# Rotary embedding on one core: tiles of 8, 8, 8, 16, 16 and 8 rows a partition, and rows dealt anew to the engines

## The chip, the cores and the metric

The kernel runs on one core of one Trainium2 chip. The metric is the device time of one execution in microseconds, the median of the runs shown; smaller is better. The profile is of one execution.

## The reference

The input `x` has 16 batches of 512 positions with 1024 numbers each, read as 16 heads of 64. Each head's halves are rotated by the angle of its position:

```python
x = x.reshape(batch, seq, num_heads, head_dim)          # 16, 512, 16, 64
x1, x2 = x[..., :32], x[..., 32:]
cos, sin = cos[None, :, None, :], sin[None, :, None, :]  # cos, sin: 512 x 32
out = concatenate([x1 * cos - x2 * sin, x1 * sin + x2 * cos], axis=-1)
```

All is float32: 33.6 MB are read and 33.6 MB written.

## The kernel before, in words

The 8192 positions are taken as 64 rows of 128 positions. A row is one 4 KB run of `x` in each of the 128 partitions, and a tile is 4 or 8 rows that lie next to each other in a partition, so that a transfer moves one piece of 16 or 32 KB for each partition. `tiles` holds two tiles of 4 rows, six of 8 and two of 4. They go through a ring `x_sb` of 40 rows; results are written over the input and stored from there.

One row `u` takes three steps (L276 to L310):

- `t1 = x * cos` by VectorE into one of three PSUM slots (L293, `mul`);
- `t2 = swapped halves of x * (-sin, sin)` into one of six SBUF buffers, by GpSimd (L257), or by VectorE for the row `V_ROW` of a tile of 8 (L286, flags `V2`);
- `t1 + t2` back into the ring, by VectorE (L304, `comb`), or for the rows flagged in `PE2` by TensorE, which adds t2 to the PSUM slot by a matmul with the identity (L224, four records a row), and ScalarE, which copies the slot into the ring (L191).

VectorE issues the multiply of row u + 1 ahead of the addition of row u (`LEAD`). It may write slot u only when the addition or ScalarE's copy of row u - 3 is done; t2 buffers come free when row u - 6 is added. Everything is ordered by semaphores written out by hand; there is no scheduler.

Of the 64 rows, 58 have their t2 made by GpSimd and 6 by VectorE; 21 are added by TensorE and ScalarE and 43 by VectorE.

Loads are issued by ScalarE (L153): the first 40 rows at once, with the two tables `cos` and `sin` behind the first load, and the other four loads each behind a given row's copy (`LAG`) and after a wait for the store that frees its place in the ring. Stores are issued by SyncE (L161) when a tile's last row is added. Both queues share the 16 DMA engines.

The tables: for tiles of 4 rows the staged `cos` and `sin` can be copied as they are (L264, L182, L183). For tiles of 8 rows a partition holds other positions, and TensorE makes the tables from the staged ones with a picking matrix (L208, two matmuls of 256 columns), which ScalarE copies for GpSimd (L186, L187). VectorE makes its own small sines from PSUM (L271, L272).

Of the kernel before, what the change touches and what calls it, by code (L numbers as in the profile page):

```python
# [6 lines left out]
def bass_split_heads_rope_kernel(  # L7
# [9 lines left out]

    batch, seq, dim = x.shape
    H = int(num_heads)
    HD = dim // H
# [3 lines left out]
    R2 = 2 * R1  # L30
    assert R1 * P == seq and R1 == 4 and batch % 2 == 0
# [8 lines left out]
    singles = (0, 1, batch - 2, batch - 1)  # L40
    tiles = [(b, R1 if b in singles else R2) for b in range(batch) if b in singles or b % 2 == 0]
    NT = len(tiles)
    RING = 5 * R2

    rows = [(t, r) for t, (_, n) in enumerate(tiles) for r in range(n)]
    NU = len(rows)
    EARLY = (NU - RING) // R2


    V_ROW = 3  # L50
    PE2 = [R1 <= u < NU - R1 and u % R2 in (1, 3, 6) for u in range(NU)]
    V2 = [tiles[t][1] == R2 and r == V_ROW for t, r in rows]

# [12 lines left out]
    LAG = 10  # L66

    with ExitStack() as stack:
# [3 lines left out]
        s1_sb = stack.enter_context(nc.sbuf_tensor([P, R1, 2, HALF], fp32))  # L72
        s2_sb = stack.enter_context(nc.sbuf_tensor([P, R2, 2, HALF], fp32))
        ident = stack.enter_context(nc.sbuf_tensor([P, P], fp32))
        pick = stack.enter_context(nc.sbuf_tensor([P, 2, 2, P // 2], fp32))
        zero = stack.enter_context(nc.sbuf_tensor([P, BANK], bf16))
        tab_ps = stack.enter_context(nc.psum_tensor([P, BANK], fp32))
        pair_ps = stack.enter_context(nc.psum_tensor([P, 2, 2, R1, HALF], fp32))
        t1_ps = stack.enter_context(nc.psum_tensor([P, NT1, H * HD], fp32))
        sem_in = [stack.enter_context(nc.semaphore(f"in{t}")) for t in range(NT)]  # L80
        sem_out = [stack.enter_context(nc.semaphore(f"out{k}")) for k in range(EARLY)]
# [3 lines left out]
        sem_c = stack.enter_context(nc.semaphore("ctab"))  # L85
        sem_s = stack.enter_context(nc.semaphore("stab"))
        sem_z = stack.enter_context(nc.semaphore("zero"))
# [7 lines left out]
        sem_t = stack.enter_context(nc.semaphore("pairs"))  # L95
        sem_a = stack.enter_context(nc.semaphore("act"))

        c1_ps = tab_ps[:, 0:R1 * HALF].rearrange("p (r d) -> p r d", d=HALF)
        v_ps = tab_ps[:, R1 * HALF:R1 * HALF + HD].rearrange("p (t d) -> p t d", d=HALF)

        def c_of(t, r):
            return c1_ps[:, r, :] if tiles[t][1] == R1 else pair_ps[:, r // R1, 0, r % R1, :]

        def s_of(t, r):
            return s1_sb[:, r] if tiles[t][1] == R1 else s2_sb[:, r]

        x1 = x.rearrange("b (s r) d -> b s (r d)", r=R1)
        o1 = out.rearrange("b (s r) h d -> b s (r h d)", r=R1)
        x2 = x.rearrange("b s d -> (b s) d").rearrange("(g p r) d -> g p (r d)", p=P, r=R2)
        o2 = out.rearrange("b s h d -> (b s) h d").rearrange("(g p r) h d -> g p (r h d)", p=P, r=R2)  # L110
        xs = x_sb[:].rearrange("p n h t d -> p n (h t d)")

        def in_dram(single, pairs, t):
            b, n = tiles[t]
            return single[b] if n == R1 else pairs[b // 2]

        def in_sbuf(t):
            b, n = tiles[t]
            k = b * R1 % RING
            return x_sb[:, k:k + n].rearrange("p n h t d -> p (n h t d)")  # L120

        def where(u):
            t, r = rows[u]
            return t, r, u % RING

# [6 lines left out]
        def wait_added(eng, u):  # L132

            if n_pe[u]:
                eng.wait_ge(sem_a, n_pe[u])
            if n_comb[u]:
                eng.wait_ge(sem_v, n_comb[u])

        def wait_t2_free(eng, u):

            if u >= NT2:
                v = u - NT2
                if PE2[v]:
                    eng.wait_ge(sem_e, n_pe[v])
                else:
                    eng.wait_ge(sem_v, n_comb[v])

        def stores_of(k):

            return sum(b * R1 // R2 == k for b, _ in tiles)  # L150

        def load(eng, t):
            eng.dma_start(in_sbuf(t), in_dram(x1, x2, t)).then_inc(sem_in[t], 16)  # L153

        def on_sync(sp):
            for u in range(NU):
                t, r, k = where(u)
                if r == tiles[t][1] - 1:
                    wait_added(sp, u)
                    k = u // R2  # L160
                    sp.dma_start(in_dram(o1, o2, t), in_sbuf(t)).then_inc(sem_out[k] if k < EARLY else sem_rest, 16)  # L161
            sp.wait_ge(sem_rest, 16 * sum(stores_of(k) for k in range(EARLY, NU // R2)))

        def on_scalar(ae):
            later = {}
            for t, (b, n) in enumerate(tiles):
                if b * R1 + n <= RING:
                    load(ae, t)
                else:

                    later.setdefault((b * R1 - RING) // R2 * R2 + R2 - 1 + LAG, []).append(t)
                if t == 0:
                    for i, (table, sem) in enumerate(((cos, sem_cos), (sin, sem_sin))):
                        ae.dma_start(stage[:, i, :], table.rearrange("(s r) d -> s (r d)", r=R1)).then_inc(sem, 16)  # L174

            ae.wait_ge(sem_i, 2)
            ae.activation(  # L177
                pick[:], ident[:].rearrange("q (s k) -> q k s", k=2)[:, :, None, :].broadcast_to([P, 2, 2, P // 2]), COPY
            ).then_inc(sem_g, 1)
            ae.wait_ge(sem_sin, 16)  # L180
            sv = stage[:, 1, :].rearrange("s (r d) -> s r d", d=HALF)
            ae.activation(s1_sb[:, :, 0, :], sv, COPY, scale=-1.0)  # L182
            ae.activation(s1_sb[:, :, 1, :], sv, COPY).then_inc(sem_s, 1)  # L183
            ae.wait_ge(sem_t, 2)
            s2 = s2_sb[:].rearrange("p (k r) t d -> p k r t d", r=R1)
            ae.activation(s2[:, :, :, 0, :], pair_ps[:, :, 1, :, :], COPY, scale=-1.0)  # L186
            ae.activation(s2[:, :, :, 1, :], pair_ps[:, :, 1, :, :], COPY).then_inc(sem_s, 1)  # L187
            for u in range(NU):
                if PE2[u]:
                    ae.wait_ge(sem_e, n_pe[u])  # L190
                    ae.activation(xs[:, u % RING, :], t1_ps[:, u % NT1, :], COPY).then_inc(sem_a, 1)  # L191
                for t in later.get(u, ()):
                    k = (tiles[t][0] * R1 - RING) // R2
                    ae.wait_ge(sem_out[k], 16 * stores_of(k))
                    load(ae, t)

        def on_tensor(pe):
# [6 lines left out]
            pe.wait_ge(sem_g, 1)  # L204
            pe.wait_ge(sem_cos, 16)
            pe.wait_ge(sem_sin, 16)
            for k in range(2):
                pe.matmul(  # L208
                    pair_ps[:, k].rearrange("p c r d -> p (c r d)"),
                    pick[:, k].rearrange("q b s -> q (b s)"),  # L210
                    stage[:].rearrange("q c f -> q (c f)"),
                    start=True,
                    stop=True,
                ).then_inc(sem_t, 1)
# [4 lines left out]

# [14 lines left out]
        def on_gpsimd(pl):  # L234
# [10 lines left out]
            ).then_inc(sem_i, 1)  # L245
            for u in range(NU):
                if V2[u]:
                    continue
                t, r, k = where(u)
                if (t, r) == (0, 0):  # L250
                    pl.wait_ge(sem_s, 1)
                if (t, r) == (2, 0):
                    pl.wait_ge(sem_s, 2)
                if r == 0:
                    pl.wait_ge(sem_in[t], 16)
                wait_t2_free(pl, u)
                pl.tensor_tensor(  # L257
                    t2_sb[:, u % NT2, :, :, :], swapped(k), over_heads(s_of(t, r)), mult
                ).then_inc(sem_p, 1)

        def on_vector(ve):
            ve.memset(zero[:], 0.0).then_inc(sem_z, 1)  # L262
            ve.wait_ge(sem_cos, 16)
            ve.tensor_copy(c1_ps, stage[:, 0, :].rearrange("s (r d) -> s r d", d=HALF)).then_inc(sem_c, 1)  # L264
            ve.wait_ge(sem_c, 1)
            ve.wait_ge(sem_w, NT1 * EH)

            def pair_tables():
                ve.wait_ge(sem_s, 2)
                row = pair_ps[:, V_ROW // R1, 1, V_ROW % R1, :]  # L270
                ve.tensor_scalar_mul(v_ps[:, 0, :], row, -1.0).then_inc(sem_c, 1)  # L271
                ve.tensor_copy(v_ps[:, 1, :], row).then_inc(sem_c, 1)  # L272

            first_v = V2.index(True)

            def mul(u):  # L276
                t, r, k = where(u)
                if r == 0:
                    ve.wait_ge(sem_in[t], 16)
                if (t, r) == (2, 0):  # L280
                    pair_tables()
                if u == first_v:
                    ve.wait_ge(sem_c, 3)
                if V2[u]:
                    wait_t2_free(ve, u)
                    ve.tensor_tensor(t2_sb[:, u % NT2, :, :, :], swapped(k), over_heads(v_ps), mult)  # L286
                if u >= NT1:
# [8 lines left out]
                    c_of(t, r)[:, None, :].broadcast_to([P, 2 * H, HALF]),  # L296
# [3 lines left out]
            def comb(u):  # L300
                t, r, k = where(u)
# [3 lines left out]
                    xs[:, k, :],  # L305
# [49 lines left out]
```

## Time and profile before

| what | value |
|---|---|
| median of 3 runs | 161.11 us (161.09 to 161.94) |
| span of the profiled execution, first to last instruction | 160.0 us |
| what lies around the span, against the median | 1.1 us |
| DMA | 67.26 MB, mean 420 GB/s over the span |
| VectorE (DVE) busy | 130.1 us, 81% |
| GpSimd (POOL) busy | 134.9 us, 84% |
| TensorE (PE) matmuls busy | 73.7 us, 46% |
| ScalarE (ACT) busy | 24.4 us, 15% |

The time of the profiled execution itself is not given apart from its span; the runs shown were timed without it. In the profile's lines, PE, PEld, DVE, ACT, POOL and SP are TensorE's matmuls and weight loads, VectorE, ScalarE, GpSimd and SyncE; L257 is line 257 of the kernel. A group's line has its busy time and the mean duration of one instruction, then the engine's idle time just before and what ended it. Durations of neighbours on an engine overlap a little, so the distance between two starts is what one costs. The DMA row gives the busy share of the 16 engines in 40 slices of 4 us, in tenths.

### The profile page before, as it was taken

The page shows a single profiled execution, that of the slowest core. Times are in us where ns is not written, and L with a number is a line of the kernel's source. Part 1 is how long each engine was busy: PE and PEld are TensorE (multiplying, and loading weights), DVE is VectorE, ACT ScalarE, POOL GpSimd, SP SyncE. Part 2 cuts the span into 40 slices and gives each one's busy share as a digit, 9 for nine tenths or more (in the row PEclk, how much of TensorE's full clock was granted, in tenths as well). Part 3 has the DMA queues.
Part 4 walks back from the last instruction along what each step waited for, and adds up shares of the span by engine and source line. Part 5 has one row for each costly group of instructions (what it writes and reads, how often), then busy time and mean ns, then how long its engine had stood idle before and what let it go on. Part 6 is the DMA issues. An engine that isn't in the chain of part 4 may idle for free.

```text
span 160.0 us, 522 instructions
## 1 busy us (share of the span) xinstructions
PE 73.7 (46%) x94; PEld 23.7 (15%) x94; DVE 130.1 (81%) x117; ACT 24.4 (15%) x27; POOL 134.9 (84%) x64
## 2 busy tenths in 40 slices
PE   6050005476427735690948606459439841970000
PEld 1020002021102220220222002002202210320000
DVE  0069998699999998997989709899999989989600
ACT  0420000205020502022022020220220122050000
POOL 1059999999999999999999999698999999289400
PEclk9999999969955865567555685855855599577555
DMA  5999999999999999999999999999999999999997
GB/s 160 401 451 463 401 430 418 410 483 406 401 463 406 494 401 401 483 426 401 467 426 418 410 467 434 401 467 393 420 463 446 418 414 418 479 410 434 414 414 303
DMA packets 3170, 67.26 MB, mean 420 GB/s; under 512 B 352, under 2 KB 608, under 8 KB 608
## 3 DMA queue, kind: packets, MB, share of 16 engines
q10 hardware_dynamic: 1728, 33.69, 49.7%
q1 hardware_dynamic: 1440, 33.56, 48.8%
q14 instruction: 2, 0.02, 0.0%
HBM read 33.69 MB, written 33.55 MB: 420 GB/s over the span
## 4 chain that ended last, share of the span: by engine, by line
DMA 59%; POOL 22%; PE 5%; DVE 3%; issue 2%; ACTq 1%; ACT 1%; DVEq 0%
DMA x_sb<-in_x_dram 41%; POOL t_sb L257 22%; DMA out_dram<-x_sb 18%; PE t_ps L224 5%; DVE x_sb L304 2%; DVE t_ps L293 1%; ACT x_sb L191 1%; ACTq L153 1%; ACTq L174 1%; DVEq L303 0%
## 5 line engine op out<-in xcount | busy, mean ns | idle before, releaser
L257 POOL TENSOR_TENSOR t_sb<-x_sb,s_sb 128x1024 f32<-128x1024 f32 x58 | 134.2, 2358 | 14.2 <-ACT s_sb L183 8.2
L224 PE MATMUL t_ps<-t_sb,ident 128*128 128x512 f32 x84 | 68.9, 973 | 62.8 <-DVE t_ps L293 37.9
L293 DVE TENSOR_TENSOR t_ps<-x_sb,pair_ps 128x1024 f32<-128x1024 f32 x48 | 57.7, 1223 | 9.7 <-ACT x_sb L191 9.7
L304 DVE TENSOR_TENSOR x_sb<-t_ps,t_sb 128x1024 f32<-128x1024 f32 x43 | 52.4, 1218 | 2.1 <-POOL t_sb L257 2.1
L191 ACT ACTIVATE x_sb<-t_ps 128x1024 f32<-128x1024 f32 x21 | 21.5, 1024 | 110.6 <-PE t_ps L224 98.9
L224 PEld LDWEIGHTS t_ps<-t_sb,ident 128*128 128x128 f32 x84 | 21.8, 286 | 109.6 <-DVE t_ps L293 70.0
L293 DVE TENSOR_TENSOR t_ps<-x_sb,tab_ps 128x1024 f32<-128x1024 f32 x16 | 19.3, 1222 | 0.5 <-ACT x_sb L191 0.5
L286 DVE TENSOR_TENSOR t_sb<-x_sb,tab_ps 128x1024 f32<-128x1024 f32 x6 | 7.3, 1212 | 0.0
L264 DVE COPY tab_ps<-stage 128x128 f32<-128x128 f32 x1 | 0.3, 295 | 7.7 <-DMA stage<-in_cos_dram 7.7
L208 PE MATMUL pair_ps<-stage,pick 128*128 128x256 f32 x4 | 2.0, 667 | 5.1 <-DMA stage<-in_sin_dram 5.1
L201 PE MATMUL t_ps<-zero 128*128 128x512 bf16 x6 | 2.7, 630 | 1.3 <-DVE zero L262 1.3
L208 PEld LDWEIGHTS pair_ps<-stage,pick 128*128 128x128 f32 x4 | 1.2, 324 | 6.2 <-issue 6.0
L177 ACT ACT_TABLE_LOAD x1 | 1.3, 1283 | 5.0 <-issue 5.0
L201 PEld LDWEIGHTS t_ps<-zero 128*128 128x128 bf16 x6 | 0.7, 138 | 2.3 <-DVE zero L262 1.2
L262 DVE MEMSET zero<- 128x256 uint32 x1 | 0.3, 272 | 0.9 <-PEq L337 0.9
L182 ACT ACTIVATE s_sb<-stage 128x128 f32<-128x128 f32 x1 | 0.3, 310 | 2.3 <-DMA stage<-in_sin_dram 2.3
L186 ACT ACTIVATE s_sb<-pair_ps 128x256 f32<-128x256 f32 x1 | 0.4, 384 | 1.7 <-PE pair_ps L208 1.7
L235 POOL MEMSET ident<- 128x128 f32 x1 | 0.2, 205 | 0.3 <-POOLq L337 0.3
L177 ACT ACTIVATE pick<-ident 128x256 f32<-128x256 f32 x1 | 0.4, 430 | 0.0
L187 ACT ACTIVATE s_sb<-pair_ps 128x256 f32<-128x256 f32 x1 | 0.4, 377 | 0.0
L237 POOL TENSOR_SCALAR_AFFINE_SELECT ident<-ident 128x128 f32<-128x128 f32 x1 | 0.3, 294 | 0.1
L337 POOL MEMSET const-float32-0.0<- 128x1 f32 x1 | 0.1, 99 | 0.3 <-issue 0.3
(6 smaller groups left out, 1.0 us busy)
## 6 DMA issues: line engine op xcount, KB each, us to landing
x_sb<-in_x_dram ACTq DMA_DIRECT2D x6, 4096.0 KB, 38.1
out_dram<-x_sb SPq DMA_DIRECT2D x6, 4096.0 KB, 25.3
x_sb<-in_x_dram ACTq DMA_DIRECT2D x4, 2048.0 KB, 22.4
out_dram<-x_sb SPq DMA_DIRECT2D x4, 2048.0 KB, 14.9
stage<-in_cos_dram ACTq DMA_DIRECT2D x1, 64.0 KB, 7.6
stage<-in_sin_dram ACTq DMA_DIRECT2D x1, 64.0 KB, 7.3
```

Source lines behind the costliest of these rows:

```text
L153: eng.dma_start(in_sbuf(t), in_dram(x1, x2, t)).then_inc(sem_in[t], 16)
L174: ae.dma_start(stage[:, i, :], table.rearrange("(s r) d -> s (r d)", r=R1)).then_inc(sem, 16)
L177: ae.activation(pick[:], ident[:].rearrange("q (s k) -> q k s", k=2)[:, :, None, :].broadcast_to([P, 2, 2, P // 2]), COPY).then_inc(sem_g, 1)
L186: ae.activation(s2[:, :, :, 0, :], pair_ps[:, :, 1, :, :], COPY, scale=-1.0)
L191: ae.activation(xs[:, u % RING, :], t1_ps[:, u % NT1, :], COPY).then_inc(sem_a, 1)
L201: pe.matmul(t1_ps[:, k, b * BANK:(b + 1) * BANK], zero[:, 0:P], zero[:], start=True, stop=True).then_inc(sem_w, 1)
L208: pe.matmul(pair_ps[:, k].rearrange("p c r d -> p (c r d)"), pick[:, k].rearrange("q b s -> q (b s)"), stage[:].rearrange("q c f -> q (c f)"),
L224: ins = pe.matmul(t1_ps[:, u % NT1, b * BANK:(b + 1) * BANK], ident[:], t2[:, b * BANK:(b + 1) * BANK], start=False, stop=True, skip_group ...
L257: pl.tensor_tensor(t2_sb[:, u % NT2, :, :, :], swapped(k), over_heads(s_of(t, r)), mult).then_inc(sem_p, 1)
L286: ve.tensor_tensor(t2_sb[:, u % NT2, :, :, :], swapped(k), over_heads(v_ps), mult)
L293: ve.tensor_tensor(t1_ps[:, u % NT1, :].rearrange("p (h d) -> p h d", d=HALF), x_sb[:, k, :, :, :].rearrange("p h t d -> p (h t) d"), c_of ...
L304: ve.tensor_tensor(xs[:, k, :], t1_ps[:, u % NT1, :], t2_sb[:, u % NT2, :, :, :].rearrange("p h t d -> p (h t d)"), add,).then_inc(sem_v, 1)
```

## The change

Tiles are now given in a list: rows, place in the ring, the pieces in which the tile is loaded and stored, and the stores that must have landed before it is loaded. The tiles have 8, 8, 8, 16, 16 and 8 rows. The first is loaded in two halves, the second tile of 16 is stored in two halves, and so is the last. The 16-row transfers have pieces of 64 KB for each partition. There are 7 loads of `x` and 8 stores, where there were 10 of each. The two late loads, of 16 and 8 rows, are issued by ScalarE behind rows 27 and 39.

All tables, for tiles of 8 and of 16 rows, are made by TensorE: 12 matmuls of 128 columns, 4 of them for the size of 8, with two picking matrices from ScalarE. The raw sines are written into the third PSUM slot of `t1_ps`, and VectorE reads its own from there, for both sizes, just before its multiply of row 2.

VectorE makes t2 for rows 3 and 6 of a tile of 8 and for rows 3 and 11 of a tile of 16, 12 in all; GpSimd makes 52. TensorE and ScalarE add every odd row from 3 to 59, 29 rows; VectorE adds 35.

```diff
-    singles = (0, 1, batch - 2, batch - 1)
-    tiles = [(b, R1 if b in singles else R2) for b in range(batch) if b in singles or b % 2 == 0]
-    RING = 5 * R2
+    TILES = (
+        (8, 0, (4, 4), (8,), ()),
+        (8, 8, (8,), (8,), ()),
+        (8, 16, (8,), (8,), ()),
+        (16, 24, (16,), (16,), ()),
+        (16, 0, (16,), (8, 8), (0, 1)),
+        (8, 16, (8,), (4, 4), (2,)),
+    )
+    RING = 40
+    BEHIND = {5: 27, 6: 39}
...
-    V_ROW = 3
-    PE2 = [R1 <= u < NU - R1 and u % R2 in (1, 3, 6) for u in range(NU)]
-    V2 = [tiles[t][1] == R2 and r == V_ROW for t, r in rows]
+    V_ROWS = {8: (3, 6), 16: (3, 11)}
+    V2 = [r in V_ROWS[TILES[t][0]] for t, r in rows]
+    PE2 = [2 <= u < NU - R1 and u % 2 == 1 for u in range(NU)]
...
+        raw_sin = {
+            n: t1_ps[:, NT1 - 1, i * BANK:i * BANK + n * HALF].rearrange("p (r d) -> p r d", d=HALF)
+            for i, n in enumerate(SIZES)
+        }
...
         def on_scalar(ae):
...
+            for n in SIZES:
+                m = n // R1
+                ae.activation(
+                    pick[n][:],
+                    ident[:].rearrange("q (s k) -> q k s", k=m)[:, :, None, :].broadcast_to([P, m, m, P // m]),
+                    COPY,
+                ).then_inc(sem_g, 1)
+            for i, n in enumerate(SIZES):
+                ae.wait_ge(sem_t, i + 1)
+                ae.activation(s_sb[n][:, :, 0, :], raw_sin[n], COPY, scale=-1.0)
+                ae.activation(s_sb[n][:, :, 1, :], raw_sin[n], COPY).then_inc(sem_s, 1)
             for u in range(NU):
                 if PE2[u]:
                     ae.wait_ge(sem_e, n_pe[u])
-                    ae.activation(xs[:, u % RING, :], t1_ps[:, u % NT1, :], COPY).then_inc(sem_a, 1)
-                for t in later.get(u, ()):
-                    k = (tiles[t][0] * R1 - RING) // R2
-                    ae.wait_ge(sem_out[k], 16 * stores_of(k))
-                    load(ae, t)
+                    ae.activation(xs[:, place_of(u), :], t1_ps[:, u % NT1, :], COPY).then_inc(sem_a, 1)
+                for i in late:
+                    if BEHIND[i] == u:
+                        for j in TILES[loads[i][0]][4]:
+                            ae.wait_ge(sem_out[j], 16)
+                        load(ae, i)
...
         def on_tensor(pe):
...
+            pe.wait_ge(sem_w, NT1 * EH)
+            for n in SIZES:
+                for c, to in enumerate((c_ps[n], raw_sin[n])):
+                    for k in range(n // R1):
+                        ins = pe.matmul(
+                            to[:, k * R1:(k + 1) * R1, :].rearrange("p r d -> p (r d)"),
+                            pick[n][:, k].rearrange("q b s -> q (b s)"),
+                            stage[:, c, :],
+                            start=c == 0,
+                            stop=True,
+                            skip_group_check=c == 1,
+                        )
+                ins.then_inc(sem_t, 1)
...
         def on_vector(ve):
             ve.memset(zero[:], 0.0).then_inc(sem_z, 1)
-            ve.wait_ge(sem_cos, 16)
-            ve.tensor_copy(c1_ps, stage[:, 0, :].rearrange("s (r d) -> s r d", d=HALF)).then_inc(sem_c, 1)
-            ve.wait_ge(sem_c, 1)
             ve.wait_ge(sem_w, NT1 * EH)
+            def own_sines():
+                ve.wait_ge(sem_s, len(SIZES))
+                for n in SIZES:
+                    v = V_ROWS[n]
+                    some = raw_sin[n][:, v[0]:v[-1] + 1:max(1, v[-1] - v[0]), :]
+                    ve.tensor_scalar_mul(v_ps[n][:, :, 0, :], some, -1.0).then_inc(sem_k, 1)
+                    ve.tensor_copy(v_ps[n][:, :, 1, :], some).then_inc(sem_k, 1)
+                ve.wait_ge(sem_k, 2 * len(SIZES))
             def mul(u):
...
+                if n not in seen:
+                    seen.add(n)
+                    ve.wait_ge(sem_t, SIZES.index(n) + 1)
+                if u == NT1 - 1:
+                    own_sines()
```

## The prediction

> **What bounds the kernel now.** I read the page, then the windows, the DMA view of two stretches, the chain, and the timeline for durations. On the page the DMA engines are busy in every slice but the first and the last:
>
> ```profile
> span 160.0 us, 522 instructions
> ...
> DMA  5999999999999999999999999999999999999997
> ```
>
> The windows (busy us of PE, PEld, DVE, ACT, POOL, then TensorE's clock, DMA share, GB/s) give the rate:
>
> ```profile
> 0.00:4.00 4.00, 2.74 (x6) 0.74 (x6) 0.27 (x1) 0.00 (x0) 0.70 (x6) 1.00 0.57 160
> ...
> 60.00:80.00 20.00, 12.56 (x15) 3.71 (x13) 18.63 (x17) 3.27 (x4) 20.00 (x10) 0.59 1.01 436
> 80.00:100.00 20.00, 10.07 (x11) 3.53 (x12) 14.50 (x14) 2.87 (x3) 19.74 (x9) 0.59 1.00 431
> ...
> 156.00:160.00 4.00, 0.00 (x0) 0.00 (x0) 0.00 (x0) 0.00 (x0) 0.00 (x0) 0.50 0.71 303
> ```
>
> At 433 GB/s (the mean of 60 to 100 us) one row of a tile (128 x 4 KB, 0.52 MB), in or out, takes 1.21 us. The first window moved 0.64 MB, 1.5 us of work, so transfers in effect begin at 2.5 us; 67.26 MB at 433 is 155.3 us; the last window falls 1.2 us short, the slowest of the 16 engines ending last. 2.5 + 155.3 + 1.2 = 159.0 of the 160.0. The bytes stay the same, so the change can gain about 1 us at most, and loses whatever time both queues stand empty. GpSimd and VectorE are close behind:
>
> ```profile
> L257 POOL TENSOR_TENSOR t_sb<-x_sb,s_sb 128x1024 f32<-128x1024 f32 x58 | 134.2, 2358 | 14.2 <-ACT s_sb L183 8.2
> ...
> L293 DVE TENSOR_TENSOR t_ps<-x_sb,pair_ps 128x1024 f32<-128x1024 f32 x48 | 57.7, 1223 | 9.7 <-ACT x_sb L191 9.7
> ```
>
> The chain ends in a load, then that load's four rows:
>
> ```profile
> 93.17 47.21 DMA x_sb<-in_x_dram
> ...
> 140.45 9.30 POOL t_sb L257 x4
> ```
>
> How the two queues share the engines is in the DMA view of 22 to 36 us (q10 loads in 32 KB pieces, q1 stores in 16 KB pieces) and of 60 to 100 us (both 32 KB):
>
> ```profile
> q10 hardware_dynamic: 143, 4.16, 71.2%
> q1 hardware_dynamic: 109, 1.79, 29.7%
> ```
>
> ```profile
> q1 hardware_dynamic: 301, 8.81, 51.2%
> q10 hardware_dynamic: 292, 8.52, 49.4%
> ```
>
> Shares go by piece size, 2.3 to 1 and about 1 to 1. Piece durations come from the timeline:
>
> ```profile
> 36.62 1.98 PE L224 MATMUL t_ps<-t_sb,ident 128*128 128x512 f32 x4 [0.18 <-DVE t_ps L293]
> ...
> 58.59 3.78 PE L224 MATMUL t_ps<-t_sb,ident 128*128 128x512 f32 x4 [3.61 <-DVE t_ps L293]
> ...
> 144.57 1.22 DVE L293 TENSOR_TENSOR t_ps<-x_sb,tab_ps 128x1024 f32<-128x1024 f32 x1
> 145.70 1.22 DVE L304 TENSOR_TENSOR x_sb<-t_ps,t_sb 128x1024 f32<-128x1024 f32 x1
> ```
>
> VectorE starts one operation every 1.13 us; GpSimd's x4 in 9.29 us gives 2.31 a row; a TensorE row takes 1.98 us at full and 3.78 at half clock, its ScalarE eviction 1.02.
>
> **Rows dealt anew.** GpSimd 58 to 52 rows (-6 x 2.31 = -13.9 us), TensorE 21 to 29, VectorE 64 + 43 + 6 = 113 operations to 64 + 35 + 12 = 111 (-2.3 us). Per 8 rows: in 8-row tiles VectorE 8 + 4 + 2 = 14 x 1.13 = 15.8 us is the limit (GpSimd 6 x 2.31 = 13.9); in a 16-row tile only two rows leave GpSimd, 7 x 2.31 = 16.2 per 8, as before. Before, 8 rows took 16.0 to 17.3 us between its stores (30.8, 46.8, 63.5, 80.8). So the pace hardly changes.
>
> **Tables.** Before, VectorE's first multiply starts at 9.19 and GpSimd's at 9.62. Now 12 matmuls of 128 columns stand ahead; the nearest row is L208, two matmuls of 256 columns in 2.05 us, so between 0.43 (cost by column) and 0.85 each (by instruction). I take 0.55, nearer the first, as the weight loads (0.32) overlap. Size 8 is ready at 9.1 + 4 x 0.55 + 0.2 = 11.5, GpSimd starts at 12.2 after two ScalarE copies of 0.38 (+2.6). Size 16 at 16.0, copies of about 0.6 each (estimated from 128, 256 and 1024 elements: 0.30, 0.38, 1.02), then four small VectorE operations: the third multiply at about 17.5 against 13.2 (+4.3; bounds +3 and +8). No transfer waits for that at first: 40 rows of loads are queued by 5 us.
>
> **Stores.** Twelve VectorE operations after 17.5 and TensorE's last row put store 0 (rows 0-7) at about 35; before, two 4-row stores went at 20.3 and 30.8. Stores 1 and 2 follow at 51 and 67. The engines stay full: loads alone until about 36 (28 rows). Of the first 40, the last 12 rows, in 64 KB pieces beside 32 KB stores, take two thirds: 12 x 1.21 x 1.5 = 22 us, so the first 16-row tile lands at 60 (1.5 us for the slowest engine, a little more than the 1.2 above). Loads and stores 0 and 1 are 56 rows, 2.5 + 67.8 = 70.3: store 2 at 67 is just in time. This is thin: tables at their upper bound put 3 us of nothing there.
>
> **The late loads on ScalarE.** They were there before. The 16-row load stands behind row 27 (about 74), when stores 0 and 1 have landed (72 to 73), so ScalarE is not held, where before the same wait held VectorE part of 9.7 us. Its issue (0.33, at worst the 1.94 us that one took before) holds only the next eviction; the 8-row load behind row 39 is alike.
>
> **One 16-row load in place of two 8-row loads.** This decides. Before, rows 40-47 landed at 92.0 and rows 48-55 at 111.3. Now no row of 40-55 is free until all 16 are in, and by then 56 rows of loads and 24 of stores have moved: 2.5 + 80 x 1.21 = 99.3, + 1.5 = 100.8. Row 39 is done at 60 + 14 x 2.31 + 4.9 = 97.2 (its TensorE row and eviction at half clock, hand-overs); its 16-row store then takes half of the engines from the load's tail, +0.5 to +3 us. Take 101.8 (bounds 100.8 and 104). VectorE and GpSimd stand idle from about 93: 9 us, as much as the 9.7 before, but now with nothing to make it up. Then 14 rows of GpSimd (32.3) and TensorE's row 55 (4.9): 139.0. The last 8 rows are VectorE's, 16 x 1.13 = 18.1, some three of them done already: +15.0, 154.0. The last 4-row store found queued stores ahead of it before and took 8.8 from issue to landing; the quickest 4-row transfer took 7.8; here 8.0: 162.0. While row 55 is awaited the transfers run out of work for 2 or 3 us, which is where the loss shows.
>
> **Sum.** 101.8 + 37.2 + 15.0 + 8.0 = 162.0 against 160.0: +2.0. The median of the runs is 161.1, 1.1 over the span; 162.0 + 1.1 = 163.1. By the bounds (100.8 to 104, and 0.5 either way for VectorE) 161.6 to 165.8, nearly all above 162.
>
> **Rivals.**
> B, no starving: TensorE runs at full clock. It would be busy 3.6 of every 4.1 us, against 12.6 of 20 at a clock of 0.59 between 60 and 80. Row 55 comes 1.8 earlier, the transfers stay full, and the end is that of the bytes, 159.0 to 160.2, so 160.1 to 161.3, say 161.0: not slower. Against it, row 39 and its store come earlier as well and delay the 16-row load by about as much. It decides if rows 40 to 63 take under 51 us from a landing near 101.
> C, larger pieces are faster. 22 to 36 us, with 16 KB stores, ran at 425 GB/s, 60 to 100 at 433. A like step from 32 to 64 KB on the 48 of 128 rows that get such pieces (two loads and a store of 16) is 1.9% of 58 us, 1.1 us: 160.0. Against it, 8 to 12 us, 16 KB loads alone, ran at 451. [...]
> D, a 64 KB piece is moved as two of 32 KB. Shares are 1 to 1, the first 16-row tile lands at 67 instead of 60, row 39 comes 7 us later, at 104, the 16-row load is issued at 81, and the queues stand empty for about 6 us: 159.6 + 6 + 1.1 = 166.7. [...]
>
> **How the numbers follow.** Forecast 0.59, B 0.23, C 0.04, D 0.14. 0.5% is 0.8 us, about what a measurement can tell; faster is below 160.3, same up to 161.9. Faster 0.04 (C), same 0.22 (B, but for a little of it), slower 0.74. The range, 161.0 to 165.5, leaves out C, the lower part of B and D.
>
> **What would show it.** After: the sixth x load landing 101 to 104 with GpSimd's and VectorE's longest waits ended by it; stores at about 35, 51, 67, 97; a DMA slice under 9 near 139 to 142; q10 to q1 at 2 to 1 while 64 KB pieces meet 32 KB. GpSimd busy 52 x 2.36 = 123. I am wrong if the slices stay at 9 to the end (B), or already dip near 80 and 102 (D).

## The result: 167.6 us, 3.9% slower, and the profile after

The changed kernel takes 167.62 us (median of 6 runs, 166.81 to 168.38) beside 161.38 for the kernel before in the same comparison: a ratio of 1.039, 95% interval 1.0365 to 1.0415. The forecast was slower, 163.1 us (161.0 to 165.5): the sign is right, the size 4.5 us short, outside the range. The profiled execution took 166.81 us, the quickest of the six, with a span of 165.6.

The page of the kernel after, its span and its DMA row:

```profile
span 165.6 us, 615 instructions
...
DMA  5999999979999888999899999999999998799995
```

A slice is 4.1 us. The engines are nearly always busy, as before; the two thin slices at 137 to 145 us are the forecast idle time. (A piece is booked whole in the slice in which it starts. The slices of 7 and 8 before 100 us come from that: laid out over their durations, the DMA records leave no idle time there, a busy share of 1.00 to 1.02 in each slice from 4 to 99 us.) But busy is not moving. The windows of the kernel after (busy us of PE, PEld, DVE, ACT and POOL, then TensorE's clock, DMA share, GB/s):

```profile
60.00:100.00 40.00, 20.28 (x36) 7.45 (x36) 31.62 (x28) 9.22 (x9) 32.41 (x14) 0.91 1.01 433
...
100.00:135.00 35.00, 16.52 (x28) 6.05 (x28) 27.90 (x25) 6.15 (x6) 29.55 (x13) 0.76 1.00 407
...
136.00:143.00 7.00, 3.95 (x5) 1.47 (x6) 4.83 (x5) 1.42 (x2) 7.00 (x4) 0.76 0.65 281
```

From 60 to 100 us they move the 433 GB/s of before; from 100 to 135 they are as busy (1.00) and move 407, where the kernel before moved 430 in the same stretch:

```profile
100.00:135.00 35.00, 20.23 (x26) 5.69 (x24) 33.88 (x31) 7.17 (x7) 32.93 (x15) 0.69 1.00 430
```

That is 35 x (1 - 407/433) = 2.1 us of work left undone by engines that never rest. Then, from 136 to 143, the queues do run dry (281): 7 x (1 - 281/433) = 2.5 us, as much as the forecast idle time of 2 or 3 us. The groups and waits of the kernel after:

```profile
L284 POOL TENSOR_TENSOR t_sb<-x_sb,sine 128x1024 f32<-128x1024 f32 x52 | 120.4, 2360 | 29.9 <-DMA x_sb<-in_x_dram 18.8
...
L326 DVE TENSOR_TENSOR t_ps<-x_sb,tab_ps 128x1024 f32<-128x1024 f32 x64 | 76.1, 1222 | 26.1 <-DMA x_sb<-in_x_dram 11.5
```

```profile
POOL t_sb L284 <- DMA x_sb<-in_x_dram: 18.8, 2, 11.2
DVE t_ps L326 <- DMA x_sb<-in_x_dram: 11.5, 2, 11.1
```

GpSimd (POOL) is no longer short of time (120.4 us busy where it was 134.2); it waits for loads. Its longest wait and VectorE's, 11 us each, are one and the same, for the second 16-row tile. The chain of the kernel after (start, duration, what):

```profile
72.76 32.63 DMA x_sb<-in_x_dram
...
105.45 24.53 POOL t_sb L284 x11
...
130.88 20.87 POOL t_sb L284 x9
```

The 16-row load is issued at 72.8 and complete at 105.4; then GpSimd makes twenty rows one behind the other, without another wait for a load, and what follows is VectorE's last operations and the last store.

### The profile page after: what moved, and what is told of

Same layout as the page of the kernel before. It is cut to its first block, busy times and chain, and to the rows that moved or that the text cites. A ratio compares the mean times of both kernels' runs of the same rounds, so it can differ in the third digit from the quotient of the medians.

```text
span 165.6 us, 615 instructions
## 1 busy us (share of the span) xinstructions
PE 77.1 (47%) x146; PEld 30.0 (18%) x146; DVE 128.1 (77%) x116; ACT 34.2 (21%) x36; POOL 121.1 (73%) x58
## 4 chain that ended last, share of the span: by engine, by line
POOL 30%; DMA 24%; DVE 18%; PE 9%; issue 8%; another core or an unknown queue 5%; ACT 1%; ACTq 0%; DVEq 0%
POOL t_sb L284 30%; DMA x_sb<-in_x_dram 20%; DVE t_ps L326 9%; DVE x_sb L336 8%; PE t_ps L251 5%; DMA stage<-in_sin_dram 4%; PE tab_ps L234 2%; PE t_ps L234 2%; DVE t_sb L314 1%; ACT x_sb L213 1%; ACT sine L208 0%; ACT sine L209 0%; ACTq L197 0%; ACTq L175 0%
## 5 line engine op out<-in xcount | busy, mean ns | idle before, releaser
L284 POOL TENSOR_TENSOR t_sb<-x_sb,sine 128x1024 f32<-128x1024 f32 x52 | 120.4, 2360 | 29.9 <-DMA x_sb<-in_x_dram 18.8
L326 DVE TENSOR_TENSOR t_ps<-x_sb,tab_ps 128x1024 f32<-128x1024 f32 x64 | 76.1, 1222 | 26.1 <-DMA x_sb<-in_x_dram 11.5
L213 ACT ACTIVATE x_sb<-t_ps 128x1024 f32<-128x1024 f32 x29 | 29.7, 1024 | 104.1 <-PE t_ps L251 104.1
L336 DVE TENSOR_TENSOR x_sb<-t_ps,t_sb 128x1024 f32<-128x1024 f32 x35 | 42.6, 1218 | 2.3 <-POOL t_sb L284 2.0
L251 PEld LDWEIGHTS t_ps<-t_sb,ident 128*128 128x128 f32 x116 | 24.0, 227 | 109.3 <-issue 58.8
L314 DVE TENSOR_TENSOR t_sb<-x_sb,tab_ps 128x1024 f32<-128x1024 f32 x12 | 14.5, 1211 | 0.0
L234 PE MATMUL tab_ps<-stage,chosen 128*128 128x128 f32 x12 | 3.1, 432 | 4.9 <-DMA stage<-in_sin_dram 4.9
L234 PEld LDWEIGHTS tab_ps<-stage,chosen 128*128 128x128 f32 x12 | 2.8, 329 | 5.8 <-issue 5.8
L234 PE MATMUL t_ps<-stage,chosen 128*128 128x128 f32 x12 | 3.0, 421 | 0.0
L234 PEld LDWEIGHTS t_ps<-stage,chosen 128*128 128x128 f32 x12 | 2.8, 333 | 0.0
```

The lines of the kernel that those rows point to most:

```text
L213: ae.activation(xs[:, place_of(u), :], t1_ps[:, u % NT1, :], COPY).then_inc(sem_a, 1)
L234: ins = pe.matmul(to[:, k * R1:(k + 1) * R1, :].rearrange("p r d -> p (r d)"), pick[n][:, k].rearrange("q b s -> q (b s)"), stage[:, c, :] ...
L251: ins = pe.matmul(t1_ps[:, u % NT1, b * BANK:(b + 1) * BANK], ident[:], t2[:, b * BANK:(b + 1) * BANK], start=False, stop=True, skip_group ...
L284: pl.tensor_tensor(t2_sb[:, u % NT2, :, :, :], swapped(place_of(u)), over_heads(s_sb[n][:, r]), mult).then_inc(sem_p, 1)
L326: ve.tensor_tensor(t1_ps[:, u % NT1, :].rearrange("p (h d) -> p h d", d=HALF), x_sb[:, k, :, :, :].rearrange("p h t d -> p (h t) d"), c_ps ...
L336: ve.tensor_tensor(xs[:, place_of(u), :], t1_ps[:, u % NT1, :], t2_sb[:, u % NT2, :, :, :].rearrange("p h t d -> p (h t d)"), add,).then_i ...
```

## The experiments

Two theories stood after the result. **Lump (T)**: the 16 rows come all at once, so nothing can be made up. **Store**: the store of tile 3 (rows 24 to 39), issued at 97.5 with 64 KB pieces, takes the engines from the loads beside it. Of 18 kernels, the first four separate the two. Medians are given with the ratio to the kernel before and its 95% interval; the median of the kernel before was 161.2 to 161.4 us in every comparison.

**e1, the late 16-row tile loaded as two 8-row loads; the store as it is.**

```diff
-        (16, 0, (16,), (8, 8), (0, 1)),
+        (16, 0, (8, 8), (8, 8), (0, 1)),
-    BEHIND = {5: 27, 6: 39}
+    BEHIND = {5: 27, 6: 27, 7: 39}
```

> The changed kernel, with the second 16-row tile loaded in two halves of 8 rows (32 KB pieces); all else as changed. Theory T (one load of 16 rows: nothing of rows 40 to 55 is free until all 16 are in): rows 40 to 47 land at 92 to 95 in place of 105.4, VectorE and GpSimd lose no 11 us there, the queues stay full, and the time is that of the bytes: 161.5 us (160.8 to 162.5) against 167.6. Rival S (the 16-row store beside the load is what costs): the second half still lands at 104 to 105 and rows 48 to 55 wait for it: 164 to 166. Rival K (tables and the rows dealt anew have made the computing itself late): at most 2 us come back, 165.5 or more.

167.2 us, 1.035 [1.0297, 1.0403]: hardly better. Rows 40 to 47 landed at 91.9, so the lump was gone, but the last load now landed as late as 136.3 and VectorE waited for that one instead (waits of e1; the transfers moved 382 GB/s from 100 to 135 us, slow as in the changed kernel):

```profile
DVE t_ps L326 <- DMA x_sb<-in_x_dram: 10.6, 1, 10.6
```

The lump alone does not explain the loss.

**e2, the 16-row store held until the 16-row load has landed.**

```diff
                 wait_added(sp, u)
+                if t == 3:
+                    sp.wait_ge(sem_in[5], 16)
```

> The changed kernel, with the 16-row store held back on SyncE until the late 16-row load has landed. Five of the 16 engines had brought their part of that load by 101.1 in the changed kernel, before the store could reach them. Theory T: the load lands at 101.3 to 102.5 on all engines, row 63 and the end move by the same 3 to 4 us: 163.5 to 164.5 us; the lump itself still costs 2 to 3 us. Rival S: the store is the whole cost: 161.0 to 162. Rival K: the end is set by computing that was late before: 166.5 or more.

162.58 us, 1.007 [1.0052, 1.0088]: one wait added, 5.0 us gained. The windows and the chain of e2:

```profile
104.00:120.00 16.00, 8.15 (x15) 3.31 (x16) 14.82 (x14) 3.07 (x3) 16.00 (x8) 0.80 1.01 438
...
132.00:139.00 7.00, 2.47 (x6) 0.68 (x4) 6.67 (x7) 2.05 (x2) 7.00 (x4) 1.00 1.03 446
```

```profile
72.59 29.99 DMA x_sb<-in_x_dram
...
102.65 24.52 POOL t_sb L286 x11
...
128.06 9.30 POOL t_sb L286 x4
```

The load lands at 102.6 in place of 105.4, the rate stays at 433 and more, and the queues are full from 132 to 139, the stretch that corresponds to the dry one. The wait moves the store from 97.5 to 102.7, behind the end of the 16-row load, and the last load is well ahead of it (4.9 pieces per engine).

**e3, the same store in two halves of 32 KB pieces, both behind row 39.**

```diff
-        (16, 24, (16,), (16,), ()),
+        (16, 24, (16,), (8, 8), ()),
-                wait_added(sp, u)
+                wait_added(sp, 39 if t == 3 else u)
```

> The changed kernel, with the 16-row store issued as two of 8 rows at the same place (behind row 39), so that its pieces are 32 KB. Theory T: beside it the tail of the 16-row load in 64 KB pieces keeps two thirds instead of half, and lands at 102.5 to 103.5: 164.5 to 166 us. If 64 KB store pieces are slow in themselves (they took 2.4 to 4.0 us in the trace), the stretch of 100 to 135 us goes back from 389-425 to 430 GB/s. If not, that stretch stays below 420. Rival K: no change, 167.6.

162.95 us, 1.0095 [1.0061, 1.0129], below both of the times that were forecast. In pieces of half the size most of the loss is gone. That points at the piece. It does not clear the store's start: the two halves were issued at 99.2 and 99.6, some 2 us later than the store of the changed kernel (97.5). f3 and f4 below settle it.

**e4, only tiles of 8 rows; tables, rows and engines as in the changed kernel.**

```diff
-        (16, 24, (16,), (16,), ()),
-        (16, 0, (16,), (8, 8), (0, 1)),
+        (8, 24, (8,), (8,), ()),
+        (8, 32, (8,), (8,), ()),
+        (8, 0, (8,), (8,), (0,)),
+        (8, 8, (8,), (8,), (1,)),
-    BEHIND = {5: 27, 6: 39}
+    BEHIND = {6: 21, 7: 27, 8: 35}
```

> The changed kernel with eight tiles of 8 rows in place of 8,8,8,16,16,8: the tables by TensorE and rows 3 and 6 of each tile on VectorE stay, all pieces are 32 KB but for the first two loads and the last two stores. Theory T: no lump, so 161.0 us (160.5 to 162), the same as before the change. Rival K: the table start and the new dealing cost by themselves: 164 or more.

161.91 us, 1.0032 [1.0018, 1.0046]. The tables, the rows dealt anew and the 8-row start together cost 0.5 us; the tiles of 16 rows cost the rest, 5.7.

**f1 (e1 and e3 together) and f2 (e1 with the store held until rows 48 to 55 have landed)** ask what the lump costs once the store is out of the way.

> Both edits at once: the second 16-row tile loaded in two halves of 8 rows, and the 16-row store issued as two of 8 rows (32 KB pieces) behind row 39. Theory W (the store in 64 KB pieces is what costs, where it meets loads: it takes two thirds of the engines from them and its own pieces become slow): no 64 KB store and no lump are left, so the transfers stay at 430 GB/s from 100 to 130 us, the last load lands near 122, and the time is 161.2 us (160.8 to 162.3). Rival H (halves are no better than the lump, since the halved load alone stayed at 167.2): 162.5 to 163.5, as with the small store alone.

> The load in two halves, and the 16-row store in 64 KB pieces held back until the second half has landed. Theory W with the engines' step in it (the 64 KB pieces are slow only where some engines write while others read, as in the changed kernel, and not where all 16 change over together, as with the held store, whose 128 pieces all took 2.42 us): 161.5 us (161.0 to 162.5), pieces of 2.42 us, the last load landing at 123 to 126. If 64 KB pieces are slow beside any load: 163 or more, with pieces over 2.6 us on average.

161.89 us, 1.003 [1.0018, 1.0042], and 161.96, 1.0046 [1.0032, 1.006]. Against e3 and e2 the lump is worth 1.1 and 0.6 us (the second pair's intervals overlap a little).

**f3 and f4 make the store's piece the only difference.** All loads have 8 rows; f3 stores rows 24 to 39 in 64 KB pieces, f4 the same rows behind the same row in two stores of 32 KB pieces.

```diff
-        (16, 24, (16,), (16,), ()),
-        (16, 0, (16,), (8, 8), (0, 1)),
+        (16, 24, (8, 8), (16,), ()),     # f4: (8, 8), (8, 8), both stores behind row 39
+        (8, 0, (8,), (8,), (0,)),
+        (8, 8, (8,), (8,), (1,)),
-    BEHIND = {5: 27, 6: 39}
+    BEHIND = {6: 21, 7: 27, 8: 35}
```

> All tiles of 8 rows but one of 16 (rows 24 to 39), which is loaded in two halves of 32 KB pieces and stored in one go in 64 KB pieces, in the middle of loads. No load is in 64 KB pieces here. Theory W: the store slows the transfers to 370 to 410 GB/s while it runs, if the engines get out of step, and holds back the loads beside it: 163 to 166 us. Rival S (share alone: the loads get a third, but nothing becomes slower): the stretch stays at 430 GB/s, the last load lands at 131 to 132, just in time for row 56: 161.5 to 162.5.

> The control for the one 64 KB store: the same kernel, with that store issued as two of 8 rows in 32 KB pieces behind row 39. Both theories: 430 GB/s throughout, last load landing near 122 to 127, 161.7 us (161.2 to 162.3), as with eight tiles of 8 rows (161.9).

f3: 166.76 us, 1.034 [1.0306, 1.0374]. f4: 161.77, 1.0031 [1.0014, 1.0048]. The stores of f4 were issued 0.6 us later (98.0 for 97.4), but in both traces the last load is 0.9 pieces per engine ahead when they begin. So at this start one store costs 5.0 us by its piece. The same 35 us in f3, then in f4:

```profile
100.00:135.00 35.00, 19.38 (x32) 6.26 (x30) 28.31 (x26) 8.19 (x8) 17.38 (x8) 0.79 1.00 385
```

```profile
100.00:135.00 35.00, 20.86 (x36) 6.70 (x35) 35.00 (x32) 9.22 (x9) 29.41 (x14) 0.90 1.01 435
```

VectorE works through all of it in f4; in f3 GpSimd works half of it. The queues' shares, from 104 to 120 us in f3 and in f4 (q1 stores, q10 loads; packets, MB, share):

```profile
q1 hardware_dynamic: 64, 4.19, 71.4%
q10 hardware_dynamic: 65, 2.10, 34.1%
```

```profile
q1 hardware_dynamic: 119, 3.74, 54.1%
q10 hardware_dynamic: 102, 3.21, 46.5%
```

Two things differ in f3. The loads get 2.10 MB of 6.29, a third, where in f4 they get 3.21 of 6.95, nearly half. And the total falls from 434 GB/s to 393. In the DMA records of f3 a 64 KB store piece takes 2.77 us in the mean and up to 3.49, where all 128 of e2 take 2.42, and the load pieces beside them take 1.36 in the mean (104 to 130 us), up to 2.36, for 1.21 in f4. The falling total is most of the 5.0 us: 35 x (1 - 385/433) = 3.9 us of work left undone by engines that are all busy (1.00).

**g1, f3 with the store held until the seventh load has landed; g3, f3 with the last load issued behind row 43, the store not held.** The theory under test (J) was that the store's pieces turn slow where it joins before the end of a load.

> The kernel with one 64 KB store among tiles of 8 rows (166.8 us), with that store held back until the load before the last has landed, near 103. Theory J (a 64 KB store is slow for as long as it meets loads if it joins in the middle of a load that is already running, and is not slow if it starts after that load's end): 128 pieces of 2.42 us, 430 GB/s from 104 to 130 us, 162.0 us (161.5 to 162.8). Rival P (a 64 KB store beside 32 KB loads is slow with any start; the two held stores of before were fast for another reason): 165 or more.

> The kernel with one 64 KB store among tiles of 8 rows (166.8 us, the store not held), with the last load moved from behind row 35 to behind row 43: the store still joins in the tail of the load before (101 to 104 us), but the last load comes some 8 us after it. Theory J: the engines are thrown out of step by that tail, pieces are slow from the moment the last load joins: 165 to 167.5. Rival O: slow as well. If it is fast (under 163), the slowness needs the last load queued right behind the running one, and neither theory holds.

g1: 161.89 us, 1.003 [1.0013, 1.0047], pieces at 2.42: a 64 KB store need cost nothing. g3: 165.29, 1.0233 [1.0191, 1.0275]; there the store joined while a load was still going, and yet 127 of its 128 pieces kept to 2.42. So J fell. In g3 no piece is slow, and the time is lost another way: its last load landed at 137.5 all the same, since the store had started three pieces per engine ahead of it and took two thirds (71 to 30 from 104 to 120 us).

**g2, e2 with the last load behind row 43, and g4, e4 with its first store in two halves.** These asked whether the store is harmless when it goes first, and whether the 0.5 us that e4 leaves comes from the first store.

> The changed kernel with the store held until the late 16-row load has landed (162.6 us), and the last load moved from behind row 39 to behind row 43, so that it is issued some 8 us after the store instead of 6 us ahead of it. Theory J: the store starts alone, with all engines together, and stays at 2.42 us a piece when the load joins: 162.6 us (162 to 163.5). Rival O (what counts is which stream leads: slow where the store is ahead of the load that it runs beside): pieces of 2.7 us and more, 165 to 167.

> Eight tiles of 8 rows (161.9 us), with the first tile stored in two halves of 4 rows, so that stores start about 6 us earlier. In the kernel of eight tiles the transfers ran at 383 GB/s from 35 to 40 us, where the first store joined the loads, 0.6 us of work lost, and the kernel before lost 0.3 us at 20 to 30. Theory: the loss at the joining is smaller, 161.5 us (161.2 to 161.9). Rival: it belongs to the joining whatever its size, 161.9 or a little more.

g2: 168.57 us, 1.0429 [1.0396, 1.0463], far from both forecasts and inconclusive: the edit left the engines half idle (210 GB/s from 100 to 105), the last load was issued only at 113.1, not 8 us after the store (102.8), and landed at 141. g4: 161.98, 1.0029 [1.0013, 1.0044], no gain; where those 0.5 us go stays open.

**h1 to h4, then i1 and i2: what makes the pieces slow.** Each shifts the 64 KB store's start, or the last load's, by a row or two of work against f3 (h4: against g3).

```diff
-                wait_added(sp, u)
+                wait_added(sp, 40 if t == 3 else u)     # h1, h4, i1; 41 in h2, i2
-    BEHIND = {6: 21, 7: 27, 8: 35}
+    BEHIND = {6: 21, 7: 27, 8: 41}                      # h3, i1; 43 in h4, i2
```

> The kernel with one 64 KB store (f3, 166.8 us, pieces 2.80 us), its store held until row 40 is added, about 2 us later. Theory Q (the place of the store's pieces against the load's decides: slow when it joins with one or two load pieces left): it joins with none or one left, so either like f3, 166 to 167 us with pieces above 2.6, or like the kernel with the store held till the landing, 161.9 and 2.42. Rival U (the queue behind, the last load waiting at once, decides): unchanged, 166 to 167 and pieces 2.7 to 2.9.

> f3 with the store held until row 41 is added, about 4 us later and so behind the end of the seventh load. Theory Q: as when it waited for the landing itself, 161.9 us (161.5 to 162.5), pieces 2.42. Rival U: still 166 to 167, pieces 2.7 to 2.9, as the last load is queued as before.

> f3 with the last load issued behind row 41 in place of row 39, the store's start unchanged (about 97). Theory Q: the store joins at the same place, so pieces are slow, 2.7 to 2.9, 165.5 to 167.5 us. Rival U: the load is not queued when the store joins, so pieces are 2.42 and only the share is lost, 163 to 165.5 us.

> g3 (last load behind row 43, store joining three load pieces before the end, pieces 2.42, 165.3 us), with the store held until row 40 is added, about 2 us later, so one or two pieces before the end as in f3. Theory Q: the pieces are now slow, above 2.6 us, and the time 166 us or more. Rival U: pieces 2.42, 164 to 165.5 us.

> f3 with the store held until row 40 and the last load issued behind row 41 in place of 35: both about 3 us later, the seventh load landed before the store joins. Theory Q2 (slow when store and last load start nearly together, the load about one piece ahead on each engine): pieces above 2.6 us again, 165 to 168 us. Rival J2 (slow only when the store joins before the end of the load ahead while another is queued): pieces 2.42, 161.7 to 163 us.

> As the last, with the store held until row 41 and the last load behind row 43: both some 5 to 6 us later than in f3; the engines stand idle for some microseconds after the seventh load. Theory Q2: pieces above 2.6 us, 166.5 to 169 us. Rival J2: pieces 2.42; the idle time alone costs 2 to 3 us, 163.5 to 165 us.

(In f3 the last load stands behind row 35, not 39 as the expectation of h3 has it.) h1: 161.76 us, 1.0036 [1.0025, 1.0048]. h2: 161.87, 1.0039 [1.0025, 1.0052]. h3: 164.62, 1.0198 [1.009, 1.0306]. h4: 165.29, 1.0239 [1.0088, 1.0391]. i1: 163.35, 1.0126 [1.0055, 1.0197]. i2: 163.09, 1.0092 [1.0051, 1.0132]. h3, h4 and i1 rest on two runs each, 1.5, 2.1 and 0.9 us apart. In h1 the store was issued 2.8 us later than in f3 (100.2 for 97.4), nothing else was edited, and 5.0 us came back (issue of the store in f3, then in h1; then the shares in h1 from 104 to 120 us):

```profile
97.39 17.42 SPq L189 DMA_DIRECT2D out_dram<-x_sb  x2
```

```profile
100.22 15.89 SPq L189 DMA_DIRECT2D out_dram<-x_sb  x2
```

```profile
q1 hardware_dynamic: 79, 5.18, 74.7%
q10 hardware_dynamic: 64, 2.10, 30.3%
```

The shares are as unequal as in f3, and nothing is lost: with the last load three pieces ahead, two thirds for the store cost nothing. h1 and h2 speak against U, which has the queued load decide; h3, with pieces at 2.43, fits U and not Q. But in h3, h4, i1 and i2 the shift missed its aim: with the load behind a later row ScalarE no longer stood for the store before it (7.5 us at row 35 in f3), the rows came sooner, and the store went at 96.1, 95.2, 95.4 and 97.6. So h3 moved more than the load, and h4, i1 and i2 did not make the case that Q and Q2 ask for. What all kernels with that store show together, counted in the DMA records as pieces per engine by which one of the two, store and last load, is ahead when the other begins:

| kernel | ahead | mean piece, us | pieces over 2.5 of 128 | us |
|---|---|---|---|---|
| f3 | load by 0.9 | 2.77 | 89 | 166.76 |
| e1 | load by 0.8 | 2.76 | 82 | 167.2 |
| after | load by 0.3, store by 1.2 | 2.63 | 32 | 167.62 |
| h1 | load by 2.9 | 2.42 | 2 | 161.76 |
| g1, f2, e2 | load by 4.9 | 2.42 | 1, 3, 0 | 161.89, 161.96, 162.58 |
| h2 | load by 5.9 | 2.42 | 1 | 161.87 |
| i2 | store by 2.1 | 2.42 | 1 | 163.09 |
| h3 | store by 2.5 | 2.43 | 6 | 164.62 |
| i1, g3, h4 | store by 3.1 | 2.42, 2.42, 2.43 | 1, 1, 5 | 163.35, 165.29, 165.29 |
| g2 | store by 6.0 | 2.52 | 20 | 168.57 |

The columns fall apart into three. Load some three pieces or more ahead: hardly a piece slow and no loss from the store. Store ahead: pieces at 2.42 (but for g2, where a whole round of 16 begun at 115.8, just before the load's first pieces at 118.7, and four after it were slow), and, g2 apart, 1.2 to 3.4 us lost against g1. There the last load began later (105.3 to 107.7 us for 100.4), got a third, and came in at 134 to 138 us. A later beginning alone cost nothing: in e4 that load began at 109.0, had 54 to 47 beside 32 KB stores, and was in at 129.1, with 161.91. The two nearly in step, the load up to a piece ahead: pieces slow. The changed kernel shows both at once. The records do not name their engine, but put end to start they make sixteen strings, one for each: nine begin store, store, load and run on at 2.4 us a store piece nearly to the end, four begin load, store, load, store and go to between 2.8 and 4.0, and three are mixed. That the step between the two decides is a pattern over fourteen kernels, not shown by an edit that brought it about; the cause beneath it is open. Two 32 KB stores at f3's point (f4) did not show it: none of their pieces took over 1.30 us.

## Why the prediction was wrong, step by step

**What held.** The bound: the transfers run at 433 GB/s and the loss comes from what they do not move. The rows dealt anew: stores 0 to 2 at 31.9, 48.5 and 63.5, some 3 us ahead of the forecast (35, 51, 67), with 16.6 and 15.1 us for 8 rows, near the 15.8 worked out. GpSimd's 120.4 us for 52 rows (123). The dry queues near 140: 2.5 us (2 or 3). The tables: GpSimd's first multiply at 11.8 and the third of VectorE's at 16.2 (12.2 and 17.5), one matmul of 128 columns 0.43 (four start in the 1.70 us from 10.76 to 12.46), the lower bound. The first 16-row tile landed at 61.8 (60). The late 16-row load was issued at 72.8 (74). The 16-row store was issued at 97.5 (97), and shares went 68 to 30 beside 32 KB pieces (104 to 120 us).

**What held in size only.** After the landing the forecast has 37.2 + 15.0 + 8.0 = 60.2 us; the trace has 142.66 - 105.4 = 37.3 to the store behind row 55, 14.9 to the last, and 8.1 to the end. The first of the three was rightly reasoned. The second agrees by luck: the forecast has VectorE's operations set the pace of the last rows, but the chain goes through GpSimd, twenty rows from 105.45 to 151.75. Row 55 is the one at about half of TensorE's clock (0.55 from 138.0 to 141.6 us; in e2 1.00 from 132 to 139; timelines of the kernel after, then of e2):

```profile
138.00 3.58 PE L251 MATMUL t_ps<-t_sb,ident 128*128 128x512 f32 x4 [2.67 <-POOL t_sb L284]
```

```profile
135.19 1.96 PE L253 MATMUL t_ps<-t_sb,ident 128*128 128x512 f32 x4 [2.68 <-POOL t_sb L286]
```

**The step that failed** is the term "its 16-row store then takes half of the engines from the load's tail, +0.5 to +3 us", and with it the landing, 101.8 (bounds 100.8 and 104). Measured: 105.4. The forecast shared out bytes as if they could be divided, and looked at the bytes alone. The load's last data pieces ended at 100.7 to 102.5, within what was forecast. But behind its data each engine has a record of 4 bytes on the load's queue, and the landing goes by these: five came at 100.7 or 100.8, eleven at 103.2 to 104.9, each behind a store piece of 2.42 us that had started first. (In e2 they came at 100.6 to 102.1.) Whether such a record waits for its queue's turn or for the store piece to be done, these records can't tell. The load has landed with the last of the sixteen: the waiting engines went on 0.5 us after it (105.4 for 104.9; in e2 102.6 for 102.1). So the landing is 3.6 late, and 105.4 + 60.2 = 165.6, the measured span.

That is enough for this kernel: after 105.4 its chain waits for no load. But taking the lump away does not bring the time back, since e1 stays at 167.2. The forecast gave the store a price in one place only, the tail of one load, at a constant 433 GB/s. There is a second, hidden behind the first in the changed kernel: the transfers beside the store are slowed (407 GB/s; 382 in e1, 385 in f3), and that, with a store that takes two thirds from a load hardly begun, brings the last load in at 136.2 for 124.4 in e2. In e1, where the first price is gone, the engines wait for that load instead. So the two stand side by side and are not to be added; holding the store (e2) or halving its pieces (e3) removes both. Against e2, where the store comes behind the 16-row load's end, the 5.0 us of span are the landing (105.4 - 102.6 = 2.8), row 55 to its store (37.3 - 35.6 = 1.7, which is TensorE at a clock of 0.55, 3.58 for 1.96), the last rows (14.9 - 15.4 = -0.6) and the last store (8.1 - 6.9 = 1.1; that others still queued held it up is likely, not shown). e2 and e3, at 162.6 and 163.0, lie within 1 us of the forecast without its store term (163.1 - 1.0 = 162.1), e2 partly by luck: its landing was 1.8 us later than the 100.8 without a store, and what followed was 2.3 us shorter than the 60.2.

**The time around the span** was 1.2 us (166.81 - 165.6; 1.1 was taken). The median lies 0.8 above the profiled run, the quickest.

**The rivals.** B: its premise came true in part, TensorE had a clock of 0.91 from 60 to 100 us (0.76 from 100 to 135). That a busier TensorE has the higher clock is not shown: it was busy 20.3 of these 40 us, and before 22.6 of the same 40 at 0.59. But row 39 hung on GpSimd's 14 rows (61.9 + 14 x 2.31 = 94.2), and after it GpSimd and VectorE stood idle for the load anyway. From the landing to the last store's issue it took 52.1 us, not under 51. C falls: 407 GB/s, not more than 433. D comes nearest in number, 166.7, by a mechanism that isn't there: each piece is a single record of 64 KB, the first 16-row tile landed at 61.8 and not 67, and shares are 2 to 1, not 1 to 1. The order of the records on a string is, for the most part, piece of one queue, piece of the other (about 205 of 218 neighbours that begin between 102 and 130 us).

## What to carry to other kernels

Where loads and stores shared the DMA engines here, the size of the piece was the weight of the queue: beside a load in 32 KB pieces, a store in 64 KB pieces had 68 to 75% of the engines' time (after, f3, h1, 104 to 120 us), one in 32 KB pieces 54% (f4). That speaks for giving the larger piece to the direction that is waited for. A store in 64 KB pieces cost nothing here when the load that the engines needed next had three pieces of lead or more (h1, h2, g1). Price a competing transfer in every load that it overlaps, by whole pieces on the slowest engine, and add one piece for the report of the load's end (2.42 us here). Ask also what binds next when one cost is taken away: in e1 a second one of the same size stood behind it. And read DMA share and GB/s side by side: 1.00 at 385 (f3) is not 1.01 at 435 (f4).

## What was not expected of the hardware

- A load's report of its end can come behind the other queue's data: in the kernel after, eleven of sixteen came 2.4 us after the data, with a 64 KB store piece between.
- A 64 KB store piece took 2.42 us beside 32 KB loads in most kernels, but 2.6 to 2.8 in the mean, up to 4.02, in three (after, e1, f3), with a total of 382 to 407 GB/s in place of 433 from 100 to 135 us, all DMA engines being busy; against f3, a start 2.8 us later (h1) removed it.
- With pieces of equal size the queues came near to equal shares (54 to 47), with 64 KB beside 32 KB 71 to 34 (f4 and f3, 104 to 120 us).
- From issue to its first piece on an engine the 16-row store took 4 us in the mean while loads were queued (after: 97.5 to 101.5; h1: 100.2 to 104.2), and 0.9 us in g2, where no load was (102.8 to 103.7): the moment of issue is not the moment at which it begins to compete.
